# A narrow load, and set-up work moved from VectorE to POOL and ScalarE, at the start of a fused decoder block

## The chip, the cores and the metric

The kernel runs on one core of one Trainium2 chip. The metric is device time in microseconds of one execution. The core has TensorE (PE, with weight loads shown apart as PEld), VectorE (DVE), ScalarE (ACT), GpSimd (POOL) and SyncE (SP), each with its own instruction queue, worked off in order. DMA transfers are issued from the queues of SP, POOL and, after the change, ScalarE.

## The reference

One layer of a hybrid decoder block on 2048 tokens of width 1024, in fp32:

```python
cond = jax.nn.silu(c)
mod = (cond @ w_ada[l] + b_ada[l])[:, None, :]
sh1, sc1, g1, sh2, sc2, g2 = jnp.split(mod, N_MOD, axis=-1)
h = rms_norm(x, norm1_g[l]) * (1 + sc1) + sh1
proj = h @ w_in[l]
gq, gk, gv, gr, glr, aq, ak, av = jnp.split(proj, split_at, axis=-1)
...
y_gla = gla_group(..., gr, gla_norm_g[l])     # ends: rms_norm(o, norm_g) * silu(r)
y_att = dilated_attention_group(qa, ka, av)
x = x + g1 * (concatenate([y_gla, y_att]) @ w_out[l])
h = rms_norm(x, norm2_g[l]) * (1 + sc2) + sh2
u = causal_depthwise_conv(h @ w_up[l], conv_w[l], conv_b[l])
u_gate, u_val = jnp.split(u, 2, axis=-1)
x = x + g2 * ((silu(u_gate) * u_val) @ w_down[l])
```

## The kernel before

The tokens are cut into four chunks of 512, the width into eight blocks of 128 (`KD`). Activations lie transposed: 128 channels on the partitions, 512 tokens along them. Each fp32 product is made of three matmuls (`mm3`, L300): every operand is split into a rounded high half and a low half, and the three are high by high, low by high and high by low.

Splitting a weight is `wslot` (L231): a raw tile is loaded (two buffers, `wraw`), ScalarE casts it to the high half `whi` (L240), and VectorE subtracts it for the low half `wlo` (L241). Splitting the activations is `norm_mod1` (L461): VectorE multiplies x by the column `G` and by `rstd` (L465), ScalarE adds the shift and rounds to `hhi` (L467), VectorE adds the shift again and subtracts the high half for `hlo` (L469).

The modulation vector has 48 columns, each a dot product of one row block of `w_ada` (128 x 1024) with `cond`. At the start 16 of them are wanted: the eight shifts, `ada(k, ...)`, and the eight scales, `ada(8 + k, ...)`. Each loads its row block (L358) and takes one or two fused multiply-and-sum instructions of VectorE (L362); `ada_end` makes the column of `G` (L371). The scales' row blocks take turns in four buffers named `big`; the first of the four has held the tanh of the condition before.

`run` (L1081) begins thus. `ada_setup` loads the condition and the tables and makes `cond`; `load_x` (L398) issues the eight input tiles of chunk 0 from SP; their squares are summed on ScalarE and VectorE and over the partitions by TensorE; then for each k the two modulation columns, one of the four first weights (`FIRST`, k below 4) and one `norm_mod1`. The first four output blocks are multiplied and stay in the four PSUM buffers `psg`. Then `consts` (L185) loads constants, masks, the gate's weights and `gB`, the norm weight of the linear attention, repeated over 128 partitions and four heads; it is used in `proj` at L552. These loads, and the first loads of chunk 1's inputs (`src`, L1117), of the later modulation rows and others, wait for the modulation columns of k = 6 (`GATE`, `gate_ins`). After this point `planned` is true: loads of weights, inputs and stores go through POOL's queue (`dq`, L173) and the remaining work of the block is interleaved by generators, with weights prepared three blocks ahead. While chunk 0 is being projected, chunk 1's inputs are squared on ScalarE (L426) and summed on VectorE (L431), three buffers `sq` in turn.

The order on each engine is not the source's: a list scheduler of the framework orders the instructions by predicted times, and can move an instruction forward or back.

Of the kernel before, what the change touches and what calls it, by code (L numbers as in the profile page):

```python
# [10 lines left out]
F32 = mybir.dt.float32  # L11
F32R = mybir.dt.float32r
U32 = mybir.dt.uint32
AF = mybir.ActivationFunctionType
ALU = mybir.AluOpType
# [4 lines left out]
P = 128  # L20
T = 512
NCH = 4
KD = 8
# [2 lines left out]
BIG = 1e30  # L26
GATE = 6
FIRST = (0, 1, 2, 3)

ORDER0 = "g0 g1 g2 g3 V0 q0 q1 W0 q2 q3 V1 q4 q5 q6 q7 W1".split()  # L30
ORDER = "W0 V0 q0 q1 q2 g0 q3 V1 q4 g1 q5 q6 g2 q7 g3 W1".split()
# [103 lines left out]
class K:  # L135
# [49 lines left out]
    def consts(self):  # L185
        nc, A = self.nc, self.A
        self.ct = self.const.tile(list(CONSTS.shape), F32, name="consts_sb")
        self.after(nc.sync.dma_start(self.ct, A["consts"]))
        n0 = len(self.loads)
        self.mk = self.cload("masks", MASKS.shape, U32)  # L190
        self.halo = self.const.tile([P, 44, 2], F32, name="halo")

        raw = self.at.tile([P, T], F32, name="graw", tag="pt", bufs=5)
        self.gw = self.const.tile([96, 256], F32R, name="gw")
        self.tie(nc.vector.memset(raw[0:96, 0:256], 0.0), self.lastmm)
        for r in (0, 32, 64):
            self.loads.append(nc.sync.dma_start(raw[r:r + 16, 0:256], A["gla_w_gate"]))
            if r < 64:
                self.loads.append(nc.sync.dma_start(raw[r + 16:r + 17, 0:256], A["gla_b_gate"]))
        nc.vector.tensor_copy(self.gw, raw[0:96, 0:256])  # L200
        nc.vector.tensor_tensor(self.gw[32:64], raw[32:64, 0:256], self.gw[32:64].bitcast(F32), op=ALU.subtract)
        self.gB = self.const.tile([P, 4, P], F32, name="gB")
        g = A["gla_norm_g"]
        self.loads.append(nc.sync.dma_start(self.gB, bass.AP(tensor=g.tensor, offset=g.offset, ap=[[0, P], [0, 4], [1, P]])))
        for ld in self.loads[n0:]:
            self.after(ld)
        self.blk = self.const.tile([P, P], F32R, name="blk")

        self.tie(nc.vector.tensor_copy(self.blk, self.C("blk")), self.lastmm)
        self.tri = self.const.tile([P, P], F32R, name="tri")  # L210
        self.tie(nc.vector.tensor_copy(self.tri, self.C("tri")), self.lastmm)
        self.st = self.const.tile([P, 4, P], F32, name="state")
        nc.vector.memset(self.st, 0.0)
        self.sb = []
        for i in range(2):
            t = self.const.tile([P, 4, P], F32, name=f"sbd{i}")
            nc.vector.memset(t, 0.0)
            self.sb.append(t)
# [11 lines left out]

    def wslot(self, src, n=1024, spare=None):  # L231
        nc = self.nc
        raw = self.wraw.tile([P, 1088], F32, name="wraw")
        self.dq.dma_start(raw[:, :n], src)  # L234
        if spare is None:
            hi = self.whi.tile([P, 1088], F32R, name="whi")
            lo = self.wlo.tile([P, 1088], F32R, name="wlo")
        else:
            hi, lo = spare[:, 0:1024], spare[:, 1024:2048]
        nc.scalar.copy(hi[:, :n], raw[:, :n])  # L240
        nc.vector.tensor_tensor(lo[:, :n], raw[:, :n], hi[:, :n].bitcast(F32), op=ALU.subtract)  # L241
        return hi, lo

    def wblock(self, src, k, m, spare=None):
# [5 lines left out]
    def plan(self):  # L250

        def proj(c):
            for o in ORDER if c else ORDER0:
# [7 lines left out]
                else:  # L261
                    b += 4 * (o[0] == "q")
                    if c or b not in FIRST:
                        yield "w_ch", (b,), KD, P
# [85 lines left out]
                break  # L350
        self.tc.add_manual_dep(inst.ins, mm.ins.name, mybir.DependencyInfo(mybir.DependencyClass.Sync, mybir.DependencyReason.DATA))

    def ada(self, b, raws):

        nc = self.nc
        n = 1024 // len(raws)
        for i, raw in enumerate(raws):
            ld = nc.sync.dma_start(raw, self.A["w_ada"][b][:, i * n:(i + 1) * n])  # L358
        yield
        m = self.mod[:, b:b + 1]  # L360
        for i, raw in enumerate(raws):
            self.last = nc.vector.tensor_tensor_reduce(raw, raw, self.cond[:, i * n:(i + 1) * n], 0.5, m if i else self.ba[:, b:b + 1], ALU.mult, ALU.add, m)  # L362
        self.ada_end(b)
# [34 lines left out]
    def load_x(self, c):  # L398
        xs = []
        for k in range(KD):  # L400
            t = self.xp.tile([P, T], F32, name="x")
            self.dq.dma_start(t, self.A["xT"][c, k])
            xs.append(t)
        return xs

# [55 lines left out]
    def norm_mod1(self, x, k, rstd, G, sh, keep=False):  # L461

        nc = self.nc
        t = self.tmp.tile([P, T], F32, name="sq", bufs=3) if keep else x
        nc.vector.scalar_tensor_tensor(t, x, G[:, k:k + 1], rstd, op0=ALU.mult, op1=ALU.mult)  # L465
        hi = self.hp.tile([P, T], F32R, name="hhi")
        nc.scalar.activation(hi, t, AF.Identity, bias=sh[:, k:k + 1])  # L467
        lo = self.hp.tile([P, T], F32R, name="hlo")
        nc.vector.scalar_tensor_tensor(lo, t, sh[:, k:k + 1], hi.bitcast(F32), op0=ALU.add, op1=ALU.subtract)  # L469
        return hi, lo  # L470


    def proj(self, c, hs, hook=None, done=()):
        nc, A, D = self.nc, self.A, self.D[c]
# [3 lines left out]
        def stage(tag=None):  # L478
            if tag:
                return self.up.tile([P, T], F32, name="stg", tag=tag)  # L480
            return self.xp.tile([P, T], F32, name="stg", tag="x")
# [47 lines left out]
        def wide(b):  # L529

            pss = [self.pg() for _ in range(4)]
            for j in range(4):
                w = self.weights("w_tokw", b, j)
                order = [(i, s) for i in range(2) for s in range(4)]
                if j == 3:

                    order.sort(key=lambda x: x[1])
                for i, s in order:
                    h, l = hs[2 * j + i]
                    tk = slice(s * P, (s + 1) * P)  # L540
                    self.mm3(pss[s], [(h[:, tk], l[:, tk])], w[i:i + 1], i == 0 and j == 0, True)
                if j < 3:
                    yield
            for s in range(4):
                off = b and put_off
                st = stage("y0" if off else None)
                if b:
                    r = stage("y1" if off else None)
                    nc.scalar.activation(st, pss[s], AF.Tanh, scale=0.5)
                    nc.scalar.copy(r, pss[s])  # L550
                    nc.vector.scalar_tensor_tensor(st, st, 1.0, r, op0=ALU.add, op1=ALU.mult)
                    nc.vector.scalar_tensor_tensor(st, st, 0.5, self.gB.rearrange("p a b -> p (a b)"), op0=ALU.mult, op1=ALU.mult)  # L552
                else:
                    nc.scalar.copy(st, pss[s])
                self.dq.dma_start(D["rg" if b else "gv"][s * P:(s + 1) * P, :], st)
            if b == 1 and hook:
                hook()
            yield
# [522 lines left out]
    def run(self):  # L1081
# [4 lines left out]
        xs = self.load_x(0)  # L1086
# [6 lines left out]
        rstd = {0: self.norm_end(acc, more=sqs)}  # L1093
        h0, ws, done = [], {}, {b: self.pg() for b in FIRST}
        spare = self.at.tile([P, 2048], F32R, name="w0", tag="kt", bufs=2)
        ring = self.at.tile([P, 2048], F32, name="ring", tag="kt", bufs=2)
        for k in range(KD):
            big = [self.at.tile([P, 1024], F32, name="wada", tag="big", bufs=4)]
            pair = [self.gp.tile([P, T], F32, name="wada", tag=t) for t in ("ghi", "glo")] if k < 5 else [ring[:, (k - 5) * 1024:(k - 4) * 1024] if k < 7 else self.at.tile([P, 1024], F32, name="wada", tag="v4", bufs=1)]
            gs = [self.ada(KD + k, big), self.ada(k, pair)]  # L1100
            for g in gs:
                next(g)
            if k < len(FIRST):
                b = FIRST[k]
                ws[b] = self.wblock(self.A["w_ch"][b], KD, P, spare if k == 3 else None)
            for g in gs:
                next(g, None)
            if k == GATE:
                self.gate_ins = self.last
            h0.append(self.norm_mod1(xs[k], k, rstd[0], self.G1, self.mod[:, 0:8]))  # L1110
        for b in FIRST:
            for k in range(KD):
                self.mm3(done[b], ws[b][k:k + 1], h0[k:k + 1], k == 0, True)
# [65 lines left out]
def pack_tok(x):  # L1179

    return x.T.reshape(KD, P, NCH, T).transpose(2, 0, 1, 3)
# [6 lines left out]
def layout(x, c, w_ada, b_ada, norm1_g, w_in, gla_w_gate, gla_b_gate, gla_norm_g, q_norm_g, k_norm_g, w_out, norm2_g, w_up, conv_w, conv_b, w_down):  # L1188
# [7 lines left out]
        xT=pack_tok(x[0]), c=c[0], tables=tabs,  # L1196
# [3 lines left out]
        w_av1=half(w[:, 2832:3088], 256)[0],  # L1200
        w_tokw=np.stack([wide(w[:, 512:1024]), wide(w[:, 1024:1536])]),
        w_ch=pack_blocks(np.concatenate([w[:, 0:512], w[:, 1552:2576]], 1), P),
        gla_w_gate=gla_w_gate[0], gla_b_gate=gla_b_gate, gla_norm_g=gla_norm_g,
        w_out=pack_blocks(w_out[0], P), w_up=pack_blocks(w_up[0], P), w_down=pack_down(w_down[0]),
    )
    return {n: np.ascontiguousarray(a) for n, a in arrs.items()}
# [16 lines left out]
```

## Time and profile before

| | |
|---|---|
| time, median of 3 runs | 2603.27 us (2602.47 to 2603.3) |
| profiled execution: span from first to last instruction | 2603.1 us |
| profiled execution: time beside the span | not given apart; the span lies inside the range of the three runs |
| mean granted TensorE clock | 0.994 |
| busy shares of the span | PE 98%, PEld 81%, DVE 74%, ACT 49%, POOL 17% |
| chain that ended last | PE 77% of the span, issue, DVE and DMA 1% each |
| HBM traffic | 339.15 MB read, 62.91 MB written, 154 GB/s over the span |

An engine's busy share is an average over the whole span. Rows of the timeline give the start in us, the duration in us, the engine, the line of the kernel, the operation, the tile written and the tiles read, and in brackets how long the engine had been idle and what ended that. `SPq` and `POOLq` are the issues of transfers. Rows of groups give the count, the busy time in us, the mean of one in ns, and the idle time before them. The granted clock is the share of TensorE's full clock that the throttle let through.

### The profile page before, as it was taken

How to read it: one execution, taken by the hardware profiler on the slowest of the kernel's cores; microseconds unless marked ns; L12 is line 12 of the kernel's file. 1: busy time of each engine (PE TensorE's matmuls, PEld its weight loads, DVE VectorE, ACT ScalarE, POOL GpSimd, SP SyncE). 2: the span in 40 equal slices, each digit the busy share in tenths (PEclk: the TensorE clock that was granted, in tenths of full speed). 3: DMA queues.
4: the chain of work that ended last, by engine and by line, in shares of the span. 5: the costliest groups of instructions: out<-in, count | busy, mean ns of one | idle time of the engine just before them, and what ended most of it. 6: DMA issues, size and time to landing. Idle time of an engine off the chain costs nothing.

```text
span 2603.1 us, 46834 instructions
## 1 busy us (share of the span) xinstructions
PE 2559.7 (98%) x18142; PEld 2104.0 (81%) x18142; DVE 1930.2 (74%) x4091; ACT 1277.7 (49%) x2626; POOL 444.4 (17%) x816
## 2 busy tenths in 40 slices
PE   5999999999999999999999999999999999999999
PEld 4888888788788888887788888878888888788887
DVE  7578877768788777777987777689777775766665
ACT  4566556656454444454545544346445453433332
POOL 1343332313210000012100000310000003100001
PEclk8999999999999999999999999999999999999999
DMA  8766675756633344455334344733443435432322
GB/s 291 242 226 234 211 236 170 239 167 201 230 108 100 123 128 122 127 174 199 123 96 139 117 134 136 252 131 114 129 140 127 143 103 189 150 103 97 96 96 84
DMA packets 164194, 405.13 MB, mean 156 GB/s; under 512 B 19154, under 2 KB 61956, under 8 KB 162692
## 3 DMA queue, kind: packets, MB, share of 16 engines
q0 software_dynamic: 88128, 308.59, 35.5%
q1 hardware_dynamic: 75844, 93.55, 11.6%
q8 instruction: 143, 2.34, 0.4%
q14 instruction: 79, 0.65, 0.1%
HBM read 339.15 MB, written 62.91 MB: 154 GB/s over the span
## 4 chain that ended last, share of the span: by engine, by line
PE 77%; issue 1%; DVE 1%; DMA 1%; ACT 0%; POOL 0%; POOLq 0%; DVEq 0%; ACTq 0%
PE psg L306 22%; PE psg L307 22%; PE psg L308 22%; PE psa L850 2%; PE psa L830 2%; PE psa L954 2%; PE psa L680 1%; PE psa L949 1%; PE psa L865 0%; PE psa L753 0%; PE psa L752 0%; PE psa L969 0%; DMA wada<-in_w_ada_dram 0%; PE psa L757 0%; PE psa L779 0%
## 5 line engine op out<-in xcount | busy, mean ns | idle before, releaser
L306 PE MATMUL psg<-hhi,whi 128*128 128x512 f32 x1992 | 782.0, 396 | 9.2 <-ACT hhi L467 5.3
L307 PE MATMUL psg<-hlo,whi 128*128 128x512 f32 x1992 | 782.9, 394 | 6.7 <-DVE hlo L469 6.5
L308 PE MATMUL psg<-hhi,wlo 128*128 128x512 f32 x1992 | 780.2, 392 | 0.7 <-DVE wlo L241 0.7
L240 ACT CAST whi<-wraw 128x1024 fp32r<-128x1024 f32 (+1 forms) x391 | 410.4, 1051 | 467.4 <-PE psg L307 363.2
L241 DVE TENSOR_TENSOR wlo<-wraw,whi 128x1024 fp32r<-128x1024 f32 (+1 forms) x391 | 478.0, 1223 | 187.2 <-ACT whi L240 181.5
L306 PEld LDWEIGHTS psg<-hhi,whi 128*128 128x128 f32 x1992 | 375.0, 189 | 95.2 <-ACT hhi L467 9.3
L307 PEld LDWEIGHTS psg<-hlo,whi 128*128 128x128 f32 x1992 | 375.3, 188 | 86.7 <-DVE hlo L469 9.6
L308 PEld LDWEIGHTS psg<-hhi,wlo 128*128 128x128 f32 x1992 | 375.5, 188 | 80.6 <-issue 1.7
L306 PE MATMUL psg<-ghi,whi 128*128 128x512 f32 x744 | 295.1, 398 | 0.0
L307 PE MATMUL psg<-glo,whi 128*128 128x512 f32 x744 | 292.1, 393 | 0.5 <-DVE glo L999 0.5
L308 PE MATMUL psg<-ghi,wlo 128*128 128x512 f32 x744 | 291.6, 392 | 0.0
L234 POOL DMA_DIRECT2D wraw<-in_w_up_dram x176 | 93.6, 532 | 982.6 <-DVE wlo L241 850.5
L1073 DVE SCALAR_TENSOR_TENSOR x<-psg,mod,x 128x512 f32<-128x512 f32 x192 | 143.2, 749 | 118.2 <-PE psg L308 115.7
L306 PE MATMUL psg<-whi,hhi 128*128 128x512 f32 (+2 forms) x512 | 172.8, 345 | 8.3 <-ACT stg L523 6.2
L308 PE MATMUL psg<-whi,hlo 128*128 128x512 f32 (+2 forms) x512 | 174.8, 345 | 0.0
L307 PE MATMUL psg<-wlo,hhi 128*128 128x512 f32 (+2 forms) x512 | 174.6, 343 | 0.1
L306 PEld LDWEIGHTS psg<-ghi,whi 128*128 128x128 f32 x744 | 139.5, 188 | 34.0 <-issue 5.3
L307 PEld LDWEIGHTS psg<-glo,whi 128*128 128x128 f32 x744 | 139.8, 188 | 30.0 <-issue 1.9
L308 PEld LDWEIGHTS psg<-ghi,wlo 128*128 128x128 f32 x744 | 139.7, 188 | 29.5 <-issue 0.7
L840 ACT ACTIVATE big<-big,nm 128x256 f32<-128x256 f32 (+1 forms) x256 | 122.4, 480 | 33.6 <-DVE nm L855 33.4
L1028 ACT ACTIVATE y<-psg,tables_sb 128x512 f32<-128x512 f32 x176 | 136.1, 776 | 4.5 <-PE psg L308 3.2
L1029 DVE SCALAR_TENSOR_TENSOR y<-psg,tables_sb,y 128x511 f32<-128x511 f32 x176 | 130.7, 743 | 3.7 <-ACT y L1028 3.6
(253 smaller groups left out, 3621.9 us busy)
## 6 DMA issues: line engine op xcount, KB each, us to landing
wraw<-in_w_up_dram POOLq DMA_DIRECT2D x176, 512.0 KB, 3.6
wraw<-in_w_down_dram POOLq DMA_DIRECT2D x88, 512.0 KB, 3.6
wraw<-in_w_ch_dram POOLq DMA_DIRECT2D x44, 512.0 KB, 4.3
v<-v SPq DMA_DIRECT2D x68, 256.0 KB, 5.6
wada<-in_w_ada_dram POOLq DMA_DIRECT2D x64, 256.0 KB, 4.8
wraw<-in_w_tokw_dram POOLq DMA_DIRECT2D x32, 512.0 KB, 4.2
wraw<-in_w_out_dram POOLq DMA_DIRECT2D x32, 512.0 KB, 4.7
sq<-in_xT_dram POOLq DMA_DIRECT2D x48, 256.0 KB, 4.9
```

Source lines behind the costliest of these rows:

```text
L234: self.dq.dma_start(raw[:, :n], src)
L240: nc.scalar.copy(hi[:, :n], raw[:, :n])
L241: nc.vector.tensor_tensor(lo[:, :n], raw[:, :n], hi[:, :n].bitcast(F32), op=ALU.subtract)
L306: nc.tensor.matmul(ps, wh, hh, start=first and k == 0, stop=False, skip_group_check=shared)
L307: nc.tensor.matmul(ps, wh, hl, start=False, stop=False, skip_group_check=shared)
L308: self.lastmm = nc.tensor.matmul(ps, wl, hh, start=False, stop=k == n - 1, skip_group_check=shared)
L830: nc.tensor.matmul(at(i, hh, z), q[H[hh], i * P:(i + 1) * P], key(H[hh], i, z), start=True, stop=True, skip_group_check=True)
L840: nc.scalar.activation(t[:, lo:hi], t[:, lo:hi], AF.Exp, bias=nm[:, hh, g, i:i + 1], scale=2.0 ** -(h + 1), accum_out=dn[:, hh, g, i:i + 1])
L850: nc.tensor.transpose(ps[:n, i * P:(i + 1) * P], part(S[hh], i), self.C("id"))
L1028: nc.scalar.activation(y, ps, AF.Identity, bias=self.cb[:, b:b + 1], scale=self.cw[:, 2, b:b + 1])
L1029: nc.vector.scalar_tensor_tensor(y[:, 1:], ps[:, :T - 1], self.cw[:, 1, b:b + 1], y[:, 1:], op0=ALU.mult, op1=ALU.add)
L1073: nc.vector.scalar_tensor_tensor(x1, ps, self.mod[:, 40 + cb:41 + cb], x1, op0=ALU.mult, op1=ALU.add)
```

## The change

Five things change, all of them at the start of the program; the matmuls and their order in the source stay as they are.

- The norm weight is handed in as 128 equal rows of 128 numbers, and `gB` is loaded as 128 x 128 instead of 128 x 4 x 128; L552 reads it four times over by a broadcast view.
- Until `planned` is true, that is for the four first weights, the low halves are subtracted on POOL instead of VectorE.
- The scale columns 1, 3 and 5 (`SUMMED`) are made by a product on POOL, a scaled copy with a running sum on ScalarE and an addition of the bias column on VectorE, instead of one instruction of VectorE.
- Chunk 0's activations are made by `norm_mod0` instead of `norm_mod1`: x times `rstd` on POOL, in place; scale, shift and rounding on ScalarE for `hhi`; scale and shift once more on ScalarE without rounding; one subtraction on VectorE for `hlo`.
- Chunk 0's input loads are issued from ScalarE's queue instead of SP's.

```diff
+SUMMED = (1, 3, 5)
...
-        self.gB = self.const.tile([P, 4, P], F32, name="gB")
-        g = A["gla_norm_g"]
-        self.loads.append(nc.sync.dma_start(self.gB, bass.AP(tensor=g.tensor, offset=g.offset, ap=[[0, P], [0, 4], [1, P]])))
+        self.gB = self.cload("gla_norm_g", (P, P))
...
+        sub = nc.vector if self.planned else nc.gpsimd
...
-        nc.vector.tensor_tensor(lo[:, :n], raw[:, :n], hi[:, :n].bitcast(F32), op=ALU.subtract)
+        sub.tensor_tensor(lo[:, :n], raw[:, :n], hi[:, :n].bitcast(F32), op=ALU.subtract)
...
-    def ada(self, b, raws):
+    def ada(self, b, raws, summed=False):
...
+        if summed:
+            raw, = raws
+            nc.gpsimd.tensor_tensor(raw, raw, self.cond, op=ALU.mult)
+            nc.scalar.activation(raw, raw, AF.Copy, scale=0.5, accum_out=m)
+            nc.vector.tensor_tensor(m, m, self.ba[:, b:b + 1], op=ALU.add)
+            raws = []
...
-            self.dq.dma_start(t, self.A["xT"][c, k])
+            (self.dq if self.planned else self.nc.scalar).dma_start(t, self.A["xT"][c, k])
...
+    def norm_mod0(self, x, k, rstd, G, sh):
+        nc = self.nc
+        nc.gpsimd.tensor_tensor(x, x, rstd, op=ALU.mult)
+        hi = self.hp.tile([P, T], F32R, name="hhi")
+        nc.scalar.activation(hi, x, AF.Identity, bias=sh[:, k:k + 1], scale=G[:, k:k + 1])
+        nc.scalar.activation(x, x, AF.Identity, bias=sh[:, k:k + 1], scale=G[:, k:k + 1])
+        lo = self.hp.tile([P, T], F32R, name="hlo")
+        nc.vector.tensor_tensor(lo, x, hi.bitcast(F32), op=ALU.subtract)
+        return hi, lo
...
-                    nc.vector.scalar_tensor_tensor(st, st, 0.5, self.gB.rearrange("p a b -> p (a b)"), op0=ALU.mult, op1=ALU.mult)
+                    heads = lambda t: t.rearrange("p (a n) -> p a n", a=4)
+                    nc.vector.scalar_tensor_tensor(heads(st), heads(st), 0.5, self.gB[:, None, :].to_broadcast([P, 4, P]), op0=ALU.mult, op1=ALU.mult)
...
-            gs = [self.ada(KD + k, big), self.ada(k, pair)]
+            gs = [self.ada(KD + k, big, k in SUMMED), self.ada(k, pair)]
...
-            h0.append(self.norm_mod1(xs[k], k, rstd[0], self.G1, self.mod[:, 0:8]))
+            h0.append(self.norm_mod0(xs[k], k, rstd[0], self.G1, self.mod[:, 0:8]))
...
-        gla_w_gate=gla_w_gate[0], gla_b_gate=gla_b_gate, gla_norm_g=gla_norm_g,
+        gla_w_gate=gla_w_gate[0], gla_b_gate=gla_b_gate, gla_norm_g=np.broadcast_to(gla_norm_g.reshape(1, P), (P, P)),
```

## The prediction

> **What bounds the kernel now.** I read the page's busy table first, then the windows of the span, then the timeline around the one long hole, then the groups of instructions of the first 62 us.
>
> ```profile
> PE 2559.7 (98%) x18142; PEld 2104.0 (81%) x18142; DVE 1930.2 (74%) x4091; ACT 1277.7 (49%) x2626; POOL 444.4 (17%) x816
> ```
>
> TensorE is busy for 98% of the span: 43.4 us of 2603.1 are left without it. So I ask where those 43 us lie. Each row below is a stretch: its length, the busy time of PE, PEld, DVE, ACT and POOL, the granted clock, the DMA share and GB/s.
>
> ```profile
> 12.40:49.80 37.40, 27.34 (x78) 17.36 (x77) 36.47 (x70) 12.43 (x16) 5.49 (x10) 0.77 0.86 322
> 49.80:55.70 5.90, 5.90 (x28) 4.88 (x26) 1.18 (x2) 0.73 (x2) 0.54 (x1) 1.00 0.94 77
> 56.20:61.70 5.50, 0.00 (x0) 0.00 (x0) 1.88 (x3) 2.77 (x5) 0.90 (x2) 0.93 0.90 319
> 61.70:67.50 5.80, 5.78 (x25) 5.78 (x26) 4.50 (x8) 4.04 (x7) 5.22 (x11) 0.50 0.84 266
> 67.50:600.00 532.50, 528.79 (x4034) 446.60 (x4034) 405.74 (x870) 323.28 (x654) 174.01 (x311) 1.00 0.65 214
> 600.00:2603.00 2003.00, 1990.30 (x13986) 1628.71 (x13982) 1474.19 (x3128) 926.49 (x1935) 258.02 (x479) 1.00 0.42 136
> ```
>
> After 67.5 us TensorE misses 3.7 + 12.7 = 16.4 us of 2535: nothing the change touches. The rest is the start. From 12.4 to 49.8 VectorE has work for 36.47 of 37.40 us, so it sets the pace there; TensorE is patchy and at a granted 0.77 of its clock. From 56.2 to 61.7 TensorE does nothing, and for 5.8 us after that it runs at 0.50. The kernel's time is therefore this: when does TensorE begin its unbroken work (now at 61.7 us), and at what clock? A start that comes one microsecond earlier is one microsecond off the end, as PE is full behind it.
>
> The timeline shows what the hole waits for:
>
> ```profile
> 46.75 0.43 SPq L204 DMA_DIRECT2D gB<-in_gla_norm_g_dram  x1
> ...
> 47.50 1.07 POOL L1119 DMA_DIRECT2D sq<-in_xT_dram  x2
> ...
> 55.69 0.39 PE L308 MATMUL psg<-hhi,w 128*128 128x512 f32 x1
> 58.89 1.29 ACT L426 ACTIVATE sq<-sq 128x512 f32<-128x512 f32 x2 [7.23 <-DMA sq<-in_xT_dram]
> ...
> 60.09 1.08 ACT L240 CAST whi<-wraw 128x1088 fp32r<-128x1088 f32 x1
> ...
> 61.08 1.08 ACT L523 ACTIVATE stg<-psg 128x512 f32<-128x512 f32 x2
> ...
> 61.72 0.59 PE L306 MATMUL psg<-whi,hhi 128*128 128x272 f32 x1 [5.64 <-ACT stg L523]
> ```
>
> The first four products end at 56.08 and hold all four psg buffers. ScalarE must empty one (L523), but its queue is in order and stands 7.23 us at L426, the square of chunk 1's second input tile, whose load was issued at 47.5. That load is slow because of a neighbour:
>
> ```profile
> sq<-in_xT_dram POOLq DMA_DIRECT2D x6, 256.0 KB, 7.8
> ...
> consts_sb<-in_consts_dram SPq DMA_DIRECT2D x1, 708.0 KB, 4.2
> ...
> gB<-in_gla_norm_g_dram SPq DMA_DIRECT2D x1, 256.0 KB, 11.7
> ```
>
> The load of gB takes 11.7 us for 256 KB, where the constants take 4.2 for 708 KB. It is written as 128 x 4 pieces of 512 bytes, all from one 512-byte row. In the window from 49.8 to 55.7 the DMA engines are 94% busy and move 77 GB/s, so they are occupied by pieces that bring nothing, and the input tiles stand behind.
>
> **The change part by part.**
>
> *Narrow gB.* A quarter of the pieces (128), each from a row of its own, 64 KB. Its cost lies between nothing and a quarter of 11.7 us (2.9); I take about 1, as at the constants' rate 64 KB is 0.4 us. The two input tiles then land as the constants do, 4 to 6 us after 47.5, thus by 53.5; ScalarE has nothing in front of L523 when the products end at 56.08, and the next matmul starts after one eviction of 0.59 us (L523's 1.08 is for two, 0.54 each) at about 56.7 instead of 61.72: 5.0 us. With a hole of 0.6 us instead of 5.64 I expect the clock to stay at 1.00, so the 5.8 us at 0.50 shrink to 2.9: another 2.9. That half is uncertain: between 0 and 2.9. L552's product with the broadcast tile keeps its 128x512 elements: no cost either way.
>
> *VectorE's load, by groups of the first 62 us (count, busy us, mean ns):*
>
> ```profile
> L362 DVE CUSTOM_DVE_ANT_0 wada<-wada,cond,tables_sb 128x1024 f32<-128x1024 f32 x9 | 11.5, 1276 | 0.3 <-DMA wada<-in_w_ada_dram 0.3
> ...
> L469 DVE SCALAR_TENSOR_TENSOR hlo<-x,mod,hhi 128x512 fp32r<-128x512 f32 x8 | 6.0, 746 | 0.1
> L465 DVE SCALAR_TENSOR_TENSOR x<-x,G,rstd 128x512 f32<-128x512 f32 x8 | 6.0, 744 | 0.0
> L467 ACT ACTIVATE hhi<-x,mod 128x512 fp32r<-128x512 f32 x8 | 5.8, 724 | 18.0 <-DVE x L465 18.0
> ...
> L431 DVE TENSOR_TENSOR rstd<-rstd,sq 128x512 f32<-128x512 f32 x6 | 4.2, 692 | 9.3 <-ACT sq L426 8.9
> ...
> L241 DVE TENSOR_TENSOR wlo<-wraw,whi 128x1024 fp32r<-128x1024 f32 x3 | 3.7, 1218 | 0.9 <-ACT whi L240 0.9
> ...
> L327 ACT ACTIVATE big<-cond 128x1024 f32<-128x1024 f32 x1 | 1.1, 1057 | 2.9 <-DMA cond<-in_c_dram 2.9
> ...
> L371 DVE SCALAR_TENSOR_TENSOR G<-mod,tables_sb 128x1 f32<-128x1 f32 x8 | 1.2, 151 | 0.0
> ...
> L615 POOL MEMSET glr<- 64x512 f32 x1 | 0.5, 546 | 0.0
> ```
>
> Taken off VectorE: the eight scalings L465, 6.0; the four low halves, 4 x 1.22 = 4.9 (the fourth writes a tile named w); three modulation rows, 3 x 1.28 = 3.8. The eight low halves L469 become a plain tensor_tensor, priced as L431: 8 x (0.746 - 0.692) = 0.4 saved. Added: three additions of one column, 3 x 0.15 = 0.5. Net 14.6 us: of VectorE's 36.5 us some 21.9 remain.
>
> Put on ScalarE: eight more activations of 0.724 (5.8), three sums over 128x1024 priced as L327 at 1.06 (3.2; the accumulator's readout, not shown in this window, I bound by 0 and 0.3 each), and the input issues below. 12.43 + 9.0 is 21.4 of 37.4 us: covered, except that one more activation, 0.72, now lies in the chain from each scale to its low half.
>
> Put on POOL: eight products of 128x512 and seven of 128x1024. No row shows a POOL product. Bounds: below, VectorE's own 0.69 and 1.22 (14.1 us in all); above, three passes at the memset's 0.546 per 512 elements, one for each operand, 1.64 and 3.28 (36.1 in all). I take two passes, 1.09 and 2.18, nearest to the memset as POOL's only row: 8 x 1.09 + 7 x 2.18 = 24.0. The Trainium skill's GPSIMD Engine Reference, section 3.1, measures 4.5 us for a two-input add of 2048 elements, about twice VectorE's; by it a 128x1024 product would be an estimated 2.2.
>
> POOL starts on this when the first whi is ready, and the last input rows land about here:
>
> ```profile
> 1.67 4.11 SPq L402 DMA_DIRECT2D x<-in_xT_dram  x8
> 4.92 1.06 ACT L327 ACTIVATE big<-cond 128x1024 f32<-128x1024 f32 x1 [2.89 <-DMA cond<-in_c_dram]
> ...
> 6.40 1.65 SPq L358 DMA_DIRECT2D wada<-in_w_ada_dram  x3
> ...
> 15.01 1.04 ACT L240 CAST whi<-wraw 128x1024 fp32r<-128x1024 f32 x1 [2.25 <-DMA wraw<-in_w_ch_dram]
> ...
> 18.34 0.63 ACT L448 ACTIVATE rstd<-rstd 128x512 f32<-128x512 f32 x1
> ...
> 27.53 0.99 SPq L358 DMA_DIRECT2D ring<-in_w_ada_dram  x2
> ...
> wada<-in_w_ada_dram SPq DMA_DIRECT2D x9, 512.0 KB, 8.2
> ...
> ring<-in_w_ada_dram SPq DMA_DIRECT2D x2, 512.0 KB, 10.5
> ```
>
> From 16.05 on POOL has 24.0 us of products and its own issues (5.5 us in the window): the last scaling is ready at about 45.5 if all of that stands ahead of it, at 40 if the issues don't. Two activations and a low half follow (2 x 0.72 + 0.69 = 2.1), then the last twelve matmuls, 12 x 0.21 = 2.5 (28 take 5.90 us in the window from 49.8). So the first four products end between 45 and 50, against 56.08.
>
> The loads are the floor under this: the last modulation rows land at 28 + 10.5 = 38.5 us; two dot products (2.55), the column, 2.1 us of splitting and 2.5 of matmuls make 46. VectorE, with 21.9 us of work, is no longer in the way.
>
> The odd rows 1, 3 and 5 now pass POOL, ScalarE and VectorE: 2.18 + 1.06 + 0.15 = 3.4 us instead of 1.28, so their buffers come free 2.1 us later, and the loads of rows 5 and 7, which follow in those of rows 1 and 3, stand that long in SP's queue with the later weights behind them. The cover is what is queued already, as a row takes 8.2 us from issue to landing; without it the cost is up to 2.1 once. I take 0. The raw weights' two buffers are held by a low half of 2.18 instead of 1.22: 1 us, 0 for the same reason.
>
> *Inputs from ScalarE's queue.* Eight issues, 4.11 us, leave SP, whose first modulation load was issued at 6.40 and can go at about 2.3. They go in front of the tanh (4.92) on ScalarE: from 0.75 to 4.9, or from 2.0 to 6.1 behind the table load. So cond comes 0 to 2.3 us later, and the inputs share the DMA engines with 4 us worth of modulation rows: rstd, at 18.97 now, may come 0 to 3 us later; I take 1.3. On the other end up to 1 us is won, as the DMA engines fill earlier. Both are inside the slack of the floor above.
>
> *What is late next.* Once the products end, chunk 1's inputs. Their loads (L1119) wait for modulation row 6 and then stand in POOL's queue, behind its products: issued about 42 to 45, landed 5 us later, then L426 and the evictions behind it: 50 to 52. That is later than the products' end, so this wait ends last. I take TensorE's unbroken work to begin at 51.3: 61.7 - 51.3 = 10.4 us won, and half of the clock's 2.9, 1.4, since a hole of 2 to 4 us may remain.
>
> **The sum.** Against the span, 2603.1: less 10.4, less 1.4, is 2591.3; the execution profiled lies 0.2 us under the median of the runs, 2603.27. The instruction order is planned from predicted times and will shift behind the start as well; in the 16.4 us of holes there I allow 3 us each way. Forecast 2592.
>
> **Rivals.**
> *Only the gB part pays (2595).* POOL's products are so slow that the products of TensorE end where they do now, 56.08: 2603.1 - 5.0 - 2.9 = 2595.2, or 2598 if the clock does not come back. For it: POOL has no row of such work, and the upper price puts its end at 16.05 + 36.1 = 52.2, with 2.1 and 2.5 behind it at 56.8. Against: that price is a bound, and the last scaling need not stand behind the last low half.
> *POOL and VectorE exclude each other (2604, the other side).* VectorE's remaining 21.9 and POOL's 24.0 would add up instead of overlapping: 12.4 + 0.9 idle + 21.9 + 24.0 = 59.2 for the last low half instead of 49.8; the matmuls behind it end 6.3 later (65.5), and the unbroken work begins at 66.1, 4.4 later than now, less the 2.9 of clock: 2604.6. At the upper price it is 2616. It is slower by over 0.2% (5.2 us, about what a measurement can tell here) once POOL needs 27.7 us or more. The trace shows POOL reading nothing beside a busy VectorE, so it neither speaks for nor against. The Trainium skill's SBUF page, section "Who interferes with whom", states just this: an instruction of VectorE with two inputs in SBUF and a GpSimd instruction that reads SBUF lock each other out for their whole length. No run here shows it yet, and by that rule the offload buys nothing and this rival is the result.
> *ScalarE holds the inputs back (2596).* If the tanh, which waits for cond until 4.92, stands ahead of the issues, the inputs start at 6 instead of 1.67, rstd comes 4.3 us later, and all that hangs on it: 2592 + 4.3. Against: the issues wait for nothing.
>
> **How the numbers follow.** Forecast 0.50 (own range 2585 to 2594); only gB 0.20; ScalarE late 0.12; exclusion 0.18, of which 0.08 beyond 2608.5. Faster by over 0.2% means below 2598.1: all of the forecast, 0.15 of the gB case (the clock comes back), 0.09 of the late ScalarE: 0.74. Slower 0.08; the rest, 0.18, the same. The range 2584 to 2604 leaves out the heavy end of the exclusion and a little below.
>
> **What would show it.** gB landing in under 4 us and no stretch of DMA at 94% with 77 GB/s; VectorE no longer full from 12.4 to 49.8 but with some 22 us; POOL products at 1.1 and 2.2 us (VectorE's two-input groups still at 0.69 and 1.28: no exclusion; stretched on either engine: exclusion); TensorE's unbroken work from about 51 and no row at 0.50 after it. The forecast is wrong if POOL's products take 3 us, or if L426 still ends last behind loads that POOL issues late.

## The result, and the profile after

The changed kernel takes 2611.24 us, the median of five runs (2610.8 to 2614.76), against 2603.09 for the kernel before; the ratio is 1.0036, 95% interval 1.0025 to 1.0048. It is slower by 8 us where I had forecast 11 us faster, and outside the range. The profiled execution took 2611.23 us, 2609.1 of them from the first to the last instruction; before, the span was 2603.1.

The same stretches as before the change, after it:

```profile
12.40:49.80 37.40, 20.14 (x35) 10.12 (x36) 37.08 (x40) 15.86 (x23) 30.90 (x15) 0.77 0.71 271
49.80:55.70 5.90, 2.48 (x7) 1.29 (x5) 5.87 (x7) 2.42 (x4) 3.96 (x4) 0.79 0.45 136
56.20:61.70 5.50, 5.19 (x15) 4.16 (x16) 3.67 (x8) 5.18 (x9) 2.88 (x6) 0.63 0.48 161
61.70:67.50 5.80, 5.80 (x28) 4.77 (x27) 3.04 (x6) 3.10 (x5) 0.84 (x2) 1.00 1.03 363
67.50:600.00 532.50, 529.80 (x3963) 447.01 (x3962) 406.70 (x871) 324.44 (x655) 180.00 (x321) 1.00 0.65 215
```

VectorE is as full as before, 37.08 of 37.40 us, but with 40 instructions where it had 70. It did not become free; its instructions became longer. TensorE has 20.14 us of work in that stretch instead of 27.34. The hole and the stretch at clock 0.50 after it are gone, as forecast. They are replaced by a start that is later altogether. I measure it by the first matmul of the block behind the first four products, the one that waited for 5.64 us before the change at 61.72:

```profile
72.67 0.39 PE L308 MATMUL psg<-hhi,w 128*128 128x512 f32 x1
72.89 0.28 PE L306 MATMUL psg<-whi,hhi 128*128 128x272 f32 x1
```

It now starts at 72.89, with no hole and at full clock: 11.2 us later, less the 2.9 us that the low clock used to cost, is 8.3. That is the loss between the medians, 8.15. The two profiled spans differ by 6.0 only, as the work behind the start is 2.3 us shorter in the changed kernel; I did not take that apart.

The groups of the first 70 us (count, busy us, mean ns):

```profile
L482 POOL TENSOR_TENSOR x<-x,rstd 128x512 f32<-128x512 f32 x8 | 13.9, 1767 | 1.1 <-ACT rstd L454 1.1
L368 DVE CUSTOM_DVE_ANT_0 wada<-wada,cond,tables_sb 128x1024 f32<-128x1024 f32 x6 | 12.8, 2146 | 0.0
...
L363 POOL TENSOR_TENSOR wada<-wada,cond 128x1024 f32<-128x1024 f32 x3 | 9.0, 2989 | 0.0
L437 DVE TENSOR_TENSOR rstd<-rstd,sq 128x512 f32<-128x512 f32 x6 | 8.2, 1372 | 2.4 <-ACT sq L432 2.1
...
L377 DVE SCALAR_TENSOR_TENSOR G<-mod,tables_sb 128x1 f32<-128x1 f32 x8 | 4.9, 623 | 0.1
```

Each of VectorE's rows answers to one shown before the change. A dot product of VectorE takes 2146 ns instead of 1276, an addition 1372 instead of 692, and a column of G, one number for each partition, 623 instead of 151. A one-column instruction has no work that could take longer, so I read these times as waits that the profile books as busy time. The timeline shows what runs beside them:

```profile
6.70 4.99 ACTq L408 DMA_DIRECT2D x<-in_xT_dram  x3
...
11.73 2.71 ACT L432 ACTIVATE sq<-x 128x512 f32<-128x512 f32 x5 [3.77 <-DMA x<-in_xT_dram]
...
15.46 2.34 POOL L241 TENSOR_TENSOR wlo<-wraw,whi 128x1024 fp32r<-128x1024 f32 x1 [4.67 <-ACT whi L240]
...
15.53 5.57 DVE L437 TENSOR_TENSOR rstd<-rstd,sq 128x512 f32<-128x512 f32 x2
17.77 2.78 POOL L363 TENSOR_TENSOR wada<-wada,cond 128x1024 f32<-128x1024 f32 x1
...
26.36 0.63 ACT L454 ACTIVATE rstd<-rstd 128x512 f32<-128x512 f32 x1
...
50.27 2.98 DVE L377 SCALAR_TENSOR_TENSOR G<-mod,tables_sb 128x1 f32<-128x1 f32 x2
50.27 0.58 POOL L234 DMA_DIRECT2D wraw<-in_w_av_dram  x1
50.87 2.35 POOL L241 TENSOR_TENSOR w<-wraw,w 128x1024 fp32r<-128x1024 f32 x1
```

Two additions that took 1.4 us before take 5.57 beside two POOL products; two columns of G take 2.98 beside a third. A second thing is seen at the top. The squares of the inputs start at 11.73 us instead of 6.41, behind the issue of the last three input loads, which stands in ScalarE's queue for 4.99 us. Together they make rstd ready at 26.99 instead of 18.97.

The narrow load did what it should: it lands in 4.5 us instead of 11.7.

```profile
gla_norm_g_sb<-in_gla_norm_g_dram SPq DMA_DIRECT2D x1, 64.0 KB, 4.5
```

### The profile page after: what moved, and what is told of

Its sections match the earlier page's. It is cut to its first block, busy times and chain, and to the rows that moved or that the text cites. A ratio compares the mean times of both kernels' runs of the same rounds, so it can differ in the third digit from the quotient of the medians.

```text
span 2609.1 us, 46850 instructions
## 1 busy us (share of the span) xinstructions
PE 2560.0 (98%) x18142; PEld 2102.0 (81%) x18142; DVE 1939.4 (74%) x4076; ACT 1286.4 (49%) x2640; POOL 477.0 (18%) x831
## 4 chain that ended last, share of the span: by engine, by line
PE 77%; issue 1%; DVE 1%; DMA 0%; ACT 0%; POOL 0%; POOLq 0%; DVEq 0%; ACTq 0%
PE psg L306 22%; PE psg L307 22%; PE psg L308 22%; PE psa L869 2%; PE psa L849 2%; PE psa L973 2%; PE psa L699 1%; PE psa L968 1%; PE psa L884 0%; PE psa L772 0%; PE psa L771 0%; PE psa L988 0%; PE psa L776 0%; DVE sq L471 0%; PE psa L798 0%
## 5 line engine op out<-in xcount | busy, mean ns | idle before, releaser
L234 POOL DMA_DIRECT2D wraw<-in_w_down_dram x88 | 46.7, 530 | 479.4 <-DVE wlo L241 394.3
```

## The experiments

Theory one: a product on POOL and an instruction of VectorE with two inputs in SBUF exclude each other (the lock, from here on), and the narrow load's gain is hidden under that loss. Its rivals: ScalarE's queue, which issues the inputs late; the longer chain over three engines; a POOL that is merely busy. In each table of times the second column is the median, the third the ratio to the kernel before with its 95% interval, and the last the start of the matmul named above, 61.72 before and 72.89 after.

**The parts alone.** Three kernels have the narrow load and one further part or none; the fourth is the changed kernel with one part undone.

```diff
 gb_only           before, + narrow gB
 x_from_sp         after,  - inputs from ScalarE's queue (back on SP)
 gb_x_act          gb_only, + inputs from ScalarE's queue
 gb_scaling_pool   gb_only, + norm_mod0
```

> The kernel before with the narrow load of the norm weight alone. Theory one (VectorE and POOL exclude each other, and the narrow load is a gain that the exclusion hides): gB no longer holds up chunk 1's inputs, the hole from 56.2 to 61.7 us shrinks to about 0.6, the row at clock 0.50 behind it goes: 2603.1 - 5.0 - 2.9 = 2595, and at least 2598. Rival (the narrow load was worth nothing, as the rest of chunk 1's loads come late anyway): 2603.

> The changed kernel with the input loads back on SP's queue. In the changed kernel the first square starts at 11.73 us (6.41 before) and rstd is ready at 26.99 (18.97 before). Theory one (exclusion alone makes the loss; POOL and VectorE are full in any case): the start of the products moves by less than the rstd, and the time stays within 2 of 2611. Rival (ScalarE's queue held the inputs back and rstd with it is the cause): 4 to 8 less, 2603 to 2607.

> Narrow load and inputs from ScalarE's queue, with no work on POOL: the changed kernel less its three POOL parts. Theory one: it is as good as the narrow load alone, give or take 2: 2594 to 2598. Rival (ScalarE's queue is the cause): rstd comes about 5 us late, 2599 to 2603, and squares start at about 11.7.

> Narrow load and the scaling by rstd on POOL (with the second activation on ScalarE), nothing else of the change. Theory one (exclusion): eight POOL products of about 1.2 to 1.8 us stand in VectorE's way instead of eight scalings of 0.74, so VectorE's stretch gets 3 to 8 us longer: 2598 to 2603, and 128x512 two-input instructions of VectorE show 1.3 us or more beside POOL's. Rival (they overlap): VectorE's stretch gets 6.4 us shorter, 2589 to 2593, VectorE's instructions keep 0.69 to 0.75.

| kernel | us | ratio | start |
|---|---|---|---|
| gb_only | 2595.94 | 0.9969 (0.9956 to 0.9981) | 55.87 |
| x_from_sp | 2616.88 | 1.0049 (1.0036 to 1.0061) | 75.56 |
| gb_x_act | 2601.79 | 0.9993 (0.9984 to 1.0001) | 62.04 |
| gb_scaling_pool | 2602.06 | 0.9995 (0.9986 to 1.0004) | 60.80 |

The narrow load alone is worth 8.2 us, 2604.1 (the kernel before on that chip) less 2595.9, with the hole gone. So the rest of the change costs some 15 us (2611.2 less 2595.9; the kernel before took 2603.1 beside the one and 2604.1 beside the other). The inputs from ScalarE's queue cost 5.9 of the narrow load's gain, at the rival's end of what I expected: that part of theory one was wrong. Not all of it is the late squares themselves: the first four products end 2.0 us later than in `gb_only` (57.7 against 55.8), and then a hole of 4.3 us follows, in which ScalarE has six squares of chunk 1's inputs in front of the first eviction of a psg buffer (L541), where `gb_only` has three. That order is the scheduler's. The scaling on POOL costs 6.1. Undoing the inputs in the changed kernel did not help, against both expectations: 5.6 us worse by the medians, 2.7 by the start. Its timeline shows the lock at its plainest:

```profile
16.65 2.36 POOL L241 TENSOR_TENSOR wlo<-wraw,whi 128x1024 fp32r<-128x1024 f32 x1
17.38 14.25 DVE L368 CUSTOM_DVE_ANT_0 wada<-wada,cond,tables_sb 128x512 f32<-128x512 f32 x1 [1.82 <-DMA wada<-in_w_ada_dram]
18.96 2.35 POOL L363 TENSOR_TENSOR wada<-wada,cond 128x1024 f32<-128x1024 f32 x1
21.26 9.81 POOL L482 TENSOR_TENSOR x<-x,rstd 128x512 f32<-128x512 f32 x8
```

One dot product of 0.75 us stands for 14.25, until the last of ten POOL products has ended. The eight scalings followed each other without a gap. In the changed kernel VectorE got a turn between POOL's products, and the eight took 13.9 us. These rows also give POOL's own price: 1.23 us (9.81 / 8) and 2.35 us.

**Reads against writes.** Two kernels put POOL work beside VectorE that nobody uses, after each pair of modulation columns: products that read two tiles, or memsets that only write.

```diff
 gb_idle_reads:   for _ in range(2): nc.gpsimd.tensor_tensor(idle, cond[:, 0:T], cond[:, T:2*T], op=ALU.mult)
 gb_idle_writes:  for _ in range(4): nc.gpsimd.memset(idle, 0.0)
```

> Narrow load alone (2595.9), with sixteen POOL products of 128x512 added that nobody uses: POOL reads two tiles and writes a scratch tile, two products after each pair of modulation rows. About 1.22 us each, 20 us in all. VectorE's own work is unchanged, and it has no slack between 12 and 50 us. Theory one (exclusion): VectorE waits for each, its stretch gets up to 20 us longer, the time 10 to 20 more: 2606 to 2616; one-column instructions of VectorE show over 1 us. Rival (the loss comes from the longer chain over three engines and from the order of work, not from a port): within 3 of 2596.

> The control of the run with idle products: 32 memsets of 128x512 on POOL (0.55 us each, 17.6 us in all) tied to the same instructions. POOL is as busy and its transfers queue as long, but it reads nothing. Theory one (exclusion through reading): within 3 of 2596. Rival (a busy POOL holds up its transfers, or writing locks too): as slow as the run with idle products.

| kernel | us | ratio | start |
|---|---|---|---|
| gb_idle_reads | 2618.47 | 1.0051 (1.0037 to 1.0065) | 72.15 |
| gb_idle_writes | 2596.64 | 0.9971 (0.9961 to 0.9981) | 56.30 |

This decides between a lock and a busy POOL. The groups (POOL's rows up to 75 us, VectorE's up to 60), first with memsets, then with products:

```profile
L1129 POOL MEMSET idle<- 128x512 f32 x32 | 17.0, 532 | 28.1 <-DVE mod L368 23.4 <-DVE G L377 3.6
...
L368 DVE CUSTOM_DVE_ANT_0 wada<-wada,cond,tables_sb 128x1024 f32<-128x1024 f32 x9 | 11.5, 1276 | 0.3 <-DMA wada<-in_w_ada_dram 0.3
```

```profile
L1129 POOL TENSOR_TENSOR idle<-cond 128x512 f32<-128x512 f32 x15 | 24.1, 1604 | 31.2 <-DVE mod L368 26.4 <-DVE G L377 4.3
...
L368 DVE CUSTOM_DVE_ANT_0 wada<-wada,cond,tables_sb 128x1024 f32<-128x1024 f32 x9 | 14.5, 1608 | 0.4 <-DMA wada<-in_w_ada_dram 0.4
...
L377 DVE SCALAR_TENSOR_TENSOR G<-mod,tables_sb 128x1 f32<-128x1 f32 x8 | 4.4, 552 | 0.0
```

With 17.0 us of writing on POOL, VectorE's dot products keep 1276 ns and the time is that of the narrow load alone. With some 20 us of reading (16 products at 1.23; the 24.1 above has waits in it), VectorE does the same work and the kernel is 22 us slower, 2.5 more than I expected at most. Of the 22, 16 lie in front of the start (72.15 against 56.30); the other 6 come behind it, and I did not take them apart. That POOL reads `cond` here, as the dot products do, is not the reason: in the changed kernel additions of rstd and sq stood beside POOL products of wraw and whi.

**The chain, and the other two parts.** `gb_scaling_vector` keeps `norm_mod0` with its second activation, but the product is VectorE's (`nc.vector.tensor_tensor(x, x, rstd, op=ALU.mult)`); `gb_low_pool` and `gb_rows_pool` add the low halves or the three rows to `gb_only`; `gb_x_three` issues only the inputs k = 0, 1, 2 from ScalarE.

> As the run with the scaling on POOL (2602.1), but the product with rstd stays on VectorE: the second ScalarE activation and the plain subtraction are kept. Theory one: what cost 6 us there was POOL's product: 2594 to 2597, at or a little under the narrow load alone, since 8 x 0.1 us leave VectorE. Rival (the additional activation in the chain from each scale to its low half costs the time): 2600 to 2603.

> Narrow load and the four low halves of weights on POOL, nothing else of the change. Four POOL products of 2.35 us instead of four of 1.22 on VectorE. Theory one (exclusion): VectorE gains 4.9 and loses up to 9.4, 0 to 5 more than the narrow load alone: 2596 to 2601. Rival (overlap): 4.9 us less for VectorE, 2591 to 2594.

> Narrow load and the three modulation rows by POOL's product and ScalarE's sum, nothing else of the change. Three POOL products of 2.35 us instead of three dot products of 1.28 and their readout on VectorE. Theory one (exclusion): VectorE gains 3.8 and loses up to 7.0: 2596 to 2600. Rival (overlap): 2592 to 2594.

> Narrow load, and only the first three input tiles issued from ScalarE; the five others stay on SP ahead of the modulation rows. With all eight on ScalarE the time was 2601.8: there the sixth to eighth issue wait for the ends of earlier loads, as SP and ScalarE share eight counters for their loads, and the squares stand behind those issues until 11.65 us. Theory one (the wait in front of an issue on ScalarE's queue is the cost): with three tiles no issue waits, squares start near 6.4 us, 2594 to 2597. Rival (the modulation rows, issued early, take the inputs' share of the DMA engines): part of the 6 us stays, 2598 to 2601.

| kernel | us | ratio | start |
|---|---|---|---|
| gb_scaling_vector | 2596.97 | 0.9974 (0.9963 to 0.9984) | 56.66 |
| gb_low_pool | 2601.92 | 0.9992 (0.9983 to 1.0001) | 61.49 |
| gb_rows_pool | 2603.76 | 1.0000 (0.9991 to 1.0009) | 62.18 |
| gb_x_three | 2595.04 | 0.9963 (0.9950 to 0.9975) | 56.47 |

The additional activation costs about 1 us, so of the scaling's 6.1 POOL's product is 5. The low halves cost 6.0, a little over what I expected; the rows 7.8, against 4 at most. Taken alone the four parts cost 25.8; together they cost 15.3, I take it because a late rstd and a locked VectorE wait at the same time.

So the longer chain is cleared for the scaling, but not for the rows. In `gb_rows_pool` the third row's product ends at 34.5 us and its sum starts at 40.4, as ScalarE's queue stands 6.45 us in front of it for a scaling. In the changed kernel that product ends at 50.3, and its sum has to wait too:

```profile
53.28 1.52 ACT L484 ACTIVATE hhi<-x,mod,G 128x512 fp32r<-128x512 f32 x2 [7.45 <-DVE G L377]
...
56.12 1.04 ACT L364 ACTIVATE wada<-wada 128x1024 f32<-128x1024 f32 x1
...
58.17 0.15 DVE L365 TENSOR_TENSOR mod<-mod,tables_sb 128x1 f32<-128x1 f32 x1
```

No run has the product on VectorE and the sum on ScalarE, so how the rows' 7.8 us divide between the lock and this chain stays open.

With three inputs on ScalarE's queue nothing is lost. The start of ScalarE's timeline, first with all eight inputs on its queue, then with three:

```profile
0.75 1.36 ACTq L408 DMA_DIRECT2D x<-in_xT_dram  x3
...
5.77 0.82 ACTq L408 DMA_DIRECT2D x<-in_xT_dram  x2
...
6.86 4.75 ACTq L408 DMA_DIRECT2D x<-in_xT_dram  x3
11.65 1.67 ACT L432 ACTIVATE sq<-x 128x512 f32<-128x512 f32 x3 [3.53 <-DMA x<-in_xT_dram]
```

```profile
0.75 1.36 ACTq L408 DMA_DIRECT2D x<-in_xT_dram  x3
...
6.52 0.61 ACT L432 ACTIVATE sq<-x 128x512 f32<-128x512 f32 x1
```

In the program as built, the sixth, seventh and eighth issue each carry a wait for an earlier load. On SP's queue such a wait stands in front of loads alone; on ScalarE's the squares stand behind it too, until 11.65 us.

**One input from PSUM.** If the lock needs two inputs in SBUF on VectorE's side, a dot product that reads the condition from PSUM should run beside POOL.

```diff
+        self.cp = [self.pa() for _ in range(2)]
+        for j in range(2):
+            nc.scalar.copy(self.cp[j], self.cond[:, j * T:(j + 1) * T])
...
-            ... tensor_tensor_reduce(raw, raw, self.cond[:, i * n:(i + 1) * n], 0.5, ...)
+            ... tensor_tensor_reduce(raw, self.cp[i], raw, 0.5, ...)     # halves of 512
```

`psum_scaling` is `gb_scaling_pool` with it, `psum_scaling_low` has the low halves on POOL as well, `psum_idle_reads` is `gb_idle_reads` with it. `psum_gate5` is `psum_scaling`, and `gb_gate5` is `gb_only`, with `GATE = 5`.

> As the run with the scaling on POOL (2602.1), but VectorE's dot products of the modulation rows read the condition from PSUM (two copies by ScalarE at the start, every row as two halves of 512), so that they have one input in SBUF only. The halves cost VectorE some 11 x 0.2 us more. Theory one, with the lock only on two inputs in SBUF: the dot products keep 0.75 us beside POOL's products, POOL's eight products take 1.22 each without waits; the loss of 6 goes: 2592 to 2598. Rival (POOL and VectorE exclude each other whatever VectorE reads): 2603 to 2606.

> The same with the four low halves of weights on POOL as well. If dot products from PSUM run beside POOL's products, VectorE loses 6.0 + 4.9 us of work for some 2 us of halved rows and few contended instructions: 2588 to 2596. Rival (exclusion whatever is read): over 2606.

> The run with sixteen unused POOL products (2618.5, against 2596.6 with memsets), with the dot products reading the condition from PSUM. Of VectorE's 36.5 us the dot products are 21.5, so beside POOL most of VectorE's work then has one input in SBUF. Theory one (lock only between two SBUF inputs on VectorE and a reading POOL): the dot products keep 0.75 us and the loss of 22 shrinks to 5 to 13, 2602 to 2610. Rival (any VectorE work is shut out, and the gain of the scaling run with PSUM had another cause): 2616 to 2622.

> The scaling on POOL with the dot products from PSUM (2598.8), with chunk 1's first loads released by modulation row 5 instead of 6. There the first four products ended at about 53.5 us, 2 earlier than with the narrow load alone, but TensorE then stood 4.2 us for chunk 1's inputs and ran on at half clock. Theory one (the port was the cost; what is left is the late inputs): loads 2 to 3 us earlier, hole under 2 us, 2592 to 2596. Rival (the early loads take the last modulation rows' share of the DMA engines): 2597 to 2600.

> The control: the narrow load alone (2595.9) with the same earlier release. There the products end at 55.87 and no hole is left, so there is nothing to gain: 2595 to 2597 by theory one. Rival (an earlier release is a gain of its own): 2592 to 2594.

| kernel | us | ratio | start |
|---|---|---|---|
| psum_scaling | 2598.80 | 0.9979 (0.9970 to 0.9988) | 57.69 |
| psum_scaling_low | 2603.64 | 0.9998 (0.9988 to 1.0007) | 61.95 |
| psum_idle_reads | 2605.71 | 1.0007 (0.9997 to 1.0016) | 63.64 |
| psum_gate5 | 2596.61 | 0.9966 (0.9953 to 0.9979) | 55.89 |
| gb_gate5 | 2599.45 | 0.9980 (0.9971 to 0.9989) | 59.53 |

The groups of `psum_idle_reads`, the dot products being L372 there:

```profile
L372 DVE CUSTOM_DVE_ANT_0 wada<-psa,wada,mod 128x512 f32<-128x512 f32 x14 | 10.3, 743 | 0.0
L372 DVE CUSTOM_DVE_ANT_0 wada<-psa,wada,tables_sb 128x512 f32<-128x512 f32 x14 | 10.0, 743 | 0.0
...
L1133 POOL TENSOR_TENSOR idle<-cond 128x512 f32<-128x512 f32 x16 | 24.6, 1536 | 27.7 <-DVE G L381 23.1 <-DVE mod L372 4.1
```

Beside the same POOL products a dot product of 512 now keeps 743 ns, and the loss falls from 22 to 9 us. Part of what is left has two inputs in SBUF still: the scalings take 1144 ns instead of 744, the low halves 893 instead of 746, the columns 334 instead of 151. Another part, some 2 us by what I expected of `psum_scaling`, is the price of working a row in halves; no run has that alone.

`psum_scaling` gets back about half of the 6 us, 0.8 short of what I expected at least, for the old reason: TensorE waits for chunk 1's inputs again.

```profile
57.69 0.59 PE L306 MATMUL psg<-whi,hhi 128*128 128x272 f32 x1 [4.22 <-ACT stg L545]
```

Its products end at 53.5, 2.3 us before those of `gb_only`, and a hole of 4.2 us follows. An earlier release of the loads makes the hole 1.06 us and gains 2.2 us, so the hole was a bound of that kernel. The same release costs the control 3.5, outside both expectations: a hole of 2.66 us opens there, with five squares in front of the first eviction instead of three. 2596.61 is 0.6 over the top of what I expected, and no better than the narrow load alone. `psum_scaling_low` missed both its forecasts: the hole there is 2.86 us, and contended instructions remain; one low half of the activations stands 3.97 us beside two low halves on POOL, and the eight take 9.8 us where 5.5 would do (8 x 0.69). I did not take the rest apart.

The best versions are the narrow load alone, 2595.94, and that with three inputs on ScalarE, 2595.04: 0.3% to 0.4% below the kernel before, and not to be told apart.

## Why the prediction was wrong

*Where the time is decided* was right. The medians follow the start of the unbroken work, with the clock behind it: less the start, 2538 to 2542 us are left in every kernel but one. The one is `gb_idle_reads`, with 2546, which stays open. Behind 67.5 us nothing decided the loss: the changed kernel is among the shortest there.

*Narrow gB* was right: 5.0 + 2.9 forecast, 8.2 measured, start 55.87 (forecast 56.7). Its landing is slower than forecast, 4.5 us where I had said under 4, and that is hidden.

*POOL's price* was near: 1.09 and 2.18 taken, 1.23 and 2.35 measured alone, 26.3 us in all instead of 24.0.

*That this work lies beside VectorE's* is the step that failed: "VectorE, with 21.9 us of work, is no longer in the way". It was in the way, because POOL's 26.3 us are not beside it but in it. I had this as the exclusion rival, with 0.18, and wrote that the trace of before neither spoke for nor against it. That was true, but a rule that no row contradicts deserved more than an assumption of overlap that no row supported either. The Trainium skill's page "SBUF — State Buffer", section "Who interferes with whom", has it as the runs show it: reads lock (2618.5), writes do not (2596.6), and one input in PSUM takes VectorE out of it (743 ns beside POOL).

*The exclusion rival's own time*, 2604.6, was 6.6 too low. The last low half was put at 59.2 and ended at 63.6. Of this, 2.3 us is POOL's price; for the rest the trace offers rstd at 26.99 instead of 18.97, which I had kept out of that rival, and the third row's sum, which ran 5.8 us after its product. Behind the last low half I put 6.3 us; it took 9.3, as three low halves came together at the end and left TensorE 41 matmuls at 0.227 us.

*Inputs from ScalarE's queue* was mis-sized: 1.3 us taken for rstd, 8.0 measured in the whole change and about 6 in `gb_x_act`, where it cost 5.9. I had the rival, a ScalarE that holds the inputs back, and gave it 0.12 only, since "the issues wait for nothing". They wait for earlier loads, and not the tanh but the last three issues did the harm.

*Chunk 1's inputs late behind POOL's products* did not happen in the changed kernel, which has no hole at the start. It happened where the products end earlier: 1.07 us in `gb_scaling_pool`, 1.89 in `gb_low_pool`, 2.15 in `gb_rows_pool`, 4.22 in `psum_scaling`. So part of what these parts cost alone is that hole.

## What to carry to other kernels

Work moved from VectorE to POOL is not off VectorE's path while both read two tiles from SBUF: price it as POOL's own duration added to VectorE's queue, and move it only if it is then shorter. Reading one operand of VectorE's side from PSUM takes that instruction out of the lock; here it bought back part of the loss, and no kernel with it beat the narrow load alone. A transfer issued from a compute engine's queue brings its waits into that queue, so issue only as many as can start at once. And measure the parts of a change alone: here one part of five was worth 8 us and the others cost 15. Alone does not mean clean, though: the scheduler's order moves with every edit, and in `gb_x_act` and `gb_gate5` part of the cost looks like that.

## What the runs showed of the hardware that I had not expected

A waiting VectorE instruction was not served in turn: in `x_from_sp` a dot product stood 14.25 us through ten POOL products, while in `gb_scaling_pool` VectorE had a turn between them. What decides between the two isn't settled here. And 512 reads of one 512-byte row hold up the DMA engines for far longer than their bytes: they take 11.7 us for 256 KB, with 77 GB/s moved from 49.8 to 55.7 us, where 128 rows of their own took 4.5 (5.5 in `gb_only`, with 323 GB/s in that stretch). The change made the reads fewer and the rows their own at once, so which of the two did it is not shown. One shared row alone need not be slow: the condition, one row of 4 KB read 128 times, lands in 4.1 us.
